# Releasing the attention units behind the first memory step, pacing them by a ScalarE clock, moving the softmax statistics off the SP queue and loading the group weights in one row

## The chip, the cores and the metric

The kernel runs on one core of a Trainium2 chip. The metric is the device time of one execution in microseconds (us); the time before is the median of three runs.

The engines are named as the profile names them: PE (TensorE, matrix multiplications), PEld (its weight loads), DVE (VectorE), ACT (ScalarE), POOL (GpSimd) and SP (SyncE, which only issues DMAs). A DMA stands on the queue of the engine that issues it: SPq, ACTq or POOLq. A queue issues in order, and an engine that reaches a DMA whose source is not ready waits there.

## The reference, cut to what matters

One layer of a decoder, 1024 positions of width 1024, in float32. The change lies in its first sub-layer:

```python
a = rmsnorm(h, g_mix[l])
proj = a @ w_in[l]                      # q, k, v, the gMLP's u and v, two gate logits
for gi, (win, dil) in enumerate(DIL_GROUPS):        # 3 groups of 4 heads, dilation 1, 4, 16
    o, lse = dilated_causal_window_attention(q[:, :, gi], k[:, :, gi], v[:, :, gi], slopes[gi], win, dil)
...
alpha = jax.nn.softmax(jnp.stack(lses), axis=0)     # weights of the three groups
y_attn = jnp.sum(alpha[..., None] * outs, axis=0)
y_sgu = spatial_gating(uv, w_sgu_spatial[l], b_sgu_spatial[l], g_sgu[l])
merged = gates[:, :, 0] * (y_attn @ w_branch_attn[l]) + gates[:, :, 1] * (y_sgu @ w_branch_sgu[l])
h = h + merged @ w_out[l]
```

The later sub-layers (cross-attention into 256 memory tokens, whose keys and values need `m @ w_kv_cross`, and a SwiGLU block) are computed by lines that the change leaves alone. Only the product with w_kv_cross is computed early, in the stretch that matters here.

## The kernel before, in words

Products that must be exact to float32 are done as three fp32r matmuls of a high and a low half (`mm3`, L168 to L171). `split` makes the halves: ACT writes the high one (L137), DVE the low one (L140).

**The order of the work** is written by the class `Order` (L40). A main generator yields (cost, latency) pairs, and its costs move a clock `now`. Up to four side chains are live; a chain may take its next step when `now` has reached the time that its last step's latency set. All engines' instructions are issued in the order so made, inside `tc.manual_schedule()` too, so that an engine that waits holds up all that stands behind it on that engine.

**The stretch from 443 to 606 us** of the span holds this work, by its PSUM tiles:
- memory keys and values, `mem_kv` (L1074 to L1100): steps 0 and 1 are `psk`, steps 2 and 3 `psv`, 96 matmuls of 256 columns each.
- attention, `attn_it` (L785 to L840): one unit is a few score blocks `psS` (L796); per block a DVE reduction with the bias (L805) and an ACT exponential in place in `T` (L807); transposes `psE` (L812), copied to `ET` by ACT and DVE in turn (L816, L818); products with v, `psO` (L827), copied to `oT` by ACT (L839). There are three groups of two head pairs. `spawn_attn` (L843) puts all units in a queue.
- `stats(g)` (L961 to L982), after the last unit of group g: two transposes `pst` (L969) of the row maxima and denominators, a DVE copy `stT` (L970), two stores to the scratch tensor `sc_d` (L974), each with four loads back as `stat` (L977), in another layout, all on SP, then POOL copies into `comb` (L981).
- `combine` (L984 to L1014): weights of the groups on DVE (L988 to L999, with one ACT exponential, L993), stored as `wt_d` (L1000); then per head pair three broadcasts `wbc` over the partitions, one half on ACTq and one on POOLq (L1006), and three multiplications of `oT` on DVE (L1007), two additions (L1008, L1009) and a split into `yAh` and `yAl`.
- the gMLP: `sgu_start` and `sgu_load` (its weights, `sguc` and `wsf`, and the scaled v, `sv`), `spatial` (L929 to L953, tile `psm`, with loads `u`), and its projection `branch_sgu` (L1018 to L1033, tile `psb`, four steps `jj` of 48 matmuls, each with gate loads `mg`).
- `branch_attn` (L1036 to L1051): tile `psa`, which needs `yAh` and `yAl`, so it stands behind `combine`; its gate loads are `sig` (L1041).

`order.join("attn%d")` lets the queued units run out. It stands behind the second `branch_sgu` step.

Of the kernel before, what the change touches and what calls it, by code (L numbers as in the profile page):

```python
# [15 lines left out]
P = 128  # L16
# [19 lines left out]
class Order:  # L36

    def __init__(self, limit):
        self.now = 0.0
        self.limit = limit
        self.live = []
        self.waiting = []
# [3 lines left out]

    def _advance(self, th):  # L50
        try:
            cost, lat = next(th[1])
            self.now += cost
            th[0] = self.now + lat
        except StopIteration:
            self.live.remove(th)

# [28 lines left out]
def tile_hybrid_dilated_attn_sgu_gated_block(  # L86
# [25 lines left out]
    nc = tc.nc  # L112
# [11 lines left out]
    def H(name, dt=F32, shape=(P, 1024)):  # L124
        return heap.tile(list(shape), dt, name=name, tag="h")
# [124 lines left out]
    order = Order(4)  # L250
# [310 lines left out]
    def load_bias():  # L561
        two = big.tile([P, 2, 1024], F32, name="bias", tag="b")
        nc.gpsimd.dma_start(two, bias_tab[:, :2048].rearrange("p (g c) -> p g c", g=2))
        one = H("bias2", shape=(P, 512))
        nc.gpsimd.dma_start(one, bias_tab[:, 2048:2560])
        bias.extend([two[:, 0], two[:, 1], one])
# [104 lines left out]
    qk, vts, oT = {}, {}, {}  # L671
# [109 lines left out]
    def attn_it(g, pr, it, st):  # L781
        if (g, pr) not in oT:
            oT[g, pr] = H("oT")
        q, k = qk[g, pr]
        vt = vts[g]  # L785
        T = W("T")
        lay = []
        c = 0
        cost = 0.0
        for hh in range(2):  # L790
            S_hd = PS("psS")
            cs = c
            for (b, kbs) in it:
                n = len(kbs) * P
                S_ps = S_hd[:, c - cs:c - cs + n]
                nc.tensor.matmul(S_ps, lhsT=q[hh * HD:(hh + 1) * HD, b * P:(b + 1) * P],  # L796
                                 rhs=k[hh * HD:(hh + 1) * HD, kbs[0] * P:kbs[0] * P + n], start=True, stop=True)
                lay.append((b, kbs, hh, c, n, S_ps))
                c += n
                cost += n / P * 0.216  # L800
        for (b, kbs, hh, c0, n, S_ps) in lay:
            h = 2 * pr + hh
            col = (g * HPG + h) * 8 + b
            bt = bias[g][:, h * P:(h + 1) * P] if g == 2 else bias[g][:, h * 256 + 256 - n:(h + 1) * 256]
            nc.vector.tensor_tensor_reduce(T[:, c0:c0 + n], S_ps, bt, op0=ALU.add, op1=ALU.min,  # L805
                                           scale=1.0, scalar=3e38, accum_out=nmx[:, col:col + 1])
            nc.scalar.activation(T[:, c0:c0 + n], T[:, c0:c0 + n], AF.Exp, bias=nmx[:, col:col + 1], scale=-1.0,  # L807
                                 accum_out=den[:, col:col + 1])
        yield cost, 3.0
        E_ps = PS("psE")  # L810
        for j in range(c // P):
            nc.tensor.transpose(E_ps[:, j * P:(j + 1) * P], T[:, j * P:(j + 1) * P], ident)  # L812
        ET = W("ET")
        st["n"] += 1
        if st["n"] % 2:
            nc.scalar.activation(ET[:, :c], E_ps[:, :c], AF.Copy)  # L816
        else:
            nc.vector.tensor_copy(ET[:, :c], E_ps[:, :c])  # L818
        yield c / P * 0.107, 1.8
        for (b, kbs, hh, c0, n, _) in sorted(lay, key=lambda l: l[0]):  # L820
            q4, ob = divmod(b, 4)
            if q4 not in st:
                st[q4] = [PS("psO"), 0]
            O = st[q4][0]
            for j, kb in enumerate(kbs):
                v = vt[kb // 4][:, (kb % 4) * 256 + (2 * pr + hh) * HD:(kb % 4) * 256 + (2 * pr + hh + 1) * HD]
                nc.tensor.matmul(O[hh * HD:(hh + 1) * HD, ob * P:(ob + 1) * P], lhsT=v,  # L827
                                 rhs=ET[:, c0 + j * P:c0 + (j + 1) * P],
                                 start=(j == 0), stop=(j == len(kbs) - 1))
            st[q4][1] += 1  # L830
            if st[q4][1] == 8:
                d = DIL[g]
                nr = max(1, d // 2)
                o = oT[g, pr].rearrange("p (i r) -> p r i", r=d)
                if d == 1:
                    o = o[:, :, q4 * 512:(q4 + 1) * 512]
                else:
                    o = o[:, q4 * nr:(q4 + 1) * nr, :]
                nc.scalar.activation(o, O.rearrange("p (r i) -> p r i", r=nr), AF.Copy)  # L839
        yield c / P * 0.2, 0.0  # L840

    def spawn_attn():
        its = [(g, pr) for g in range(GROUPS) for pr in range(2)]  # L843
# [76 lines left out]
    def sgu_load():  # L920
        for half in range(2):
            nc.gpsimd.dma_start(vt_s[half], sv_d[4 * half:4 * half + 4].rearrange("b i c -> i b c"))
# [32 lines left out]
    sc_d = dram.tile([GROUPS, 2, HPG, S], F32, name="sc_d")  # L955
    wt_d = dram.tile([GROUPS, HPG, S], F32, name="wt_d")

    def comb(i):
        return consts_["comb"][:64, i * 64:(i + 1) * 64]

    def stats(g):  # L961
        while order.busy("attn%d" % g):
            yield 0.0, 1.0
        if g == 0:
            consts_["comb"] = H("comb")
        ps = PS("pst")
        stT = W("stT")
        for w_, t in enumerate((nmx, den)):
            nc.tensor.transpose(ps[:32, w_ * P:(w_ + 1) * P], t[:, g * 32:(g + 1) * 32], ident)  # L969
        nc.vector.tensor_copy(stT[:32, :256], ps[:32, :256])  # L970
        d = DIL[g]
        stat = W("stat")
        for w_ in range(2):
            nc.sync.dma_start(sc_d[g, w_].rearrange("h (b q) -> (h b) q", q=P), stT[:32, w_ * P:(w_ + 1) * P])  # L974
            src = sc_d[g, w_].rearrange("h (r c i) -> h c r i", r=d, i=64 // d)
            for h in range(HPG):
                nc.sync.dma_start(  # L977
                    stat[h * 16:(h + 1) * 16, w_ * 64:(w_ + 1) * 64].rearrange("p (r i) -> p r i", r=d), src[h])
        yield 0.22, 0.0
        for w_ in range(2):  # L980
            nc.gpsimd.tensor_copy(comb(3 * w_ + g).rearrange("p (i r) -> p i r", r=d),  # L981
                                  stat[:64, w_ * 64:(w_ + 1) * 64].rearrange("p (r i) -> p i r", r=d))  # L982

    def combine():  # L984
        while order.busy("stats"):
            yield 0.0, 1.0
        low, tot = comb(6), comb(7)
        nc.vector.tensor_tensor(low, comb(0), comb(1), op=ALU.min)  # L988
        nc.vector.tensor_tensor(low, low, comb(2), op=ALU.min)
        for g in range(3):  # L990
            nc.vector.tensor_sub(comb(g), low, comb(g))
        n_, dn_ = [consts_["comb"][:64, i * 192:(i + 1) * 192] for i in range(2)]
        nc.scalar.activation(n_, n_, AF.Exp)  # L993
        nc.vector.tensor_mul(dn_, dn_, n_)
        nc.vector.tensor_add(tot, comb(3), comb(4))
        nc.vector.tensor_add(tot, tot, comb(5))
        nc.vector.reciprocal(low, tot)
        for g in range(3):
            nc.vector.tensor_mul(comb(g), comb(g), low)  # L999
            nc.scalar.dma_start(wt_d[g].rearrange("h (c i) -> (h c) i", i=64), comb(g))  # L1000
        for pr in range(2):
            for g in range(3):
                t = H("wbc")
                for hh in range(2):
                    src = wt_d[g, 2 * pr + hh:2 * pr + hh + 1, :]
                    (nc.scalar, nc.gpsimd)[hh].dma_start(t[hh * HD:(hh + 1) * HD, :], src.to_broadcast([HD, S]))  # L1006
                nc.vector.tensor_mul(oT[g, pr], oT[g, pr], t)  # L1007
            nc.vector.tensor_add(oT[0, pr], oT[0, pr], oT[1, pr])  # L1008
            nc.vector.tensor_add(oT[0, pr], oT[0, pr], oT[2, pr])  # L1009
            y = H("yAh", F32R), H("yAl", F32R)  # L1010
            split(oT[0, pr], *y)
            yA.append(y)
            yield 0.0, 0.0
# [522 lines left out]
    def main():  # L1536
# [15 lines left out]
        with tc.manual_schedule():  # L1552
            load_qk(0, 0)
            load_bias()
            yield from mem_kv(0)
            sgu_load()
            yield from mem_kv(1)
            load_qk(0, 1)
            order.spawn(sgu_start(), key="sgu")
            yield from mem_kv(2)  # L1560
            spawn_attn()
            yield from mem_kv(3)
        sgu_norm()
        order.join("sgu")
        yield from spatial()
        for jj in range(2):
            yield from branch_sgu(jj)
        for g in range(GROUPS):
            order.join("attn%d" % g)
        for jj in range(2, 4):  # L1570
            yield from branch_sgu(jj)
        order.join("combine")
        yield from branch_attn()
# [73 lines left out]
```

## Time and profile before

| what | value |
|---|---|
| median of three runs | 1486.52 us (1485.7 to 1486.54) |
| the profiled execution's own time | 1485.01 us |
| its span | 1483.2 us |
| PE busy | 1445.8 us, 97% of the span |
| DVE, ACT, POOL busy | 993.5, 609.2, 143.4 us |
| DMA moved | 211.78 MB, mean 143 GB/s |
| chain that ended last | PE 84%, DVE 7%, DMA 5%, ACT 2% |

The span is the time from the first to the last instruction of the profiled execution. The chain is followed back from the last instruction, at each step to what released it. A share of the span is an average over stages: the stretch of this change is 163 us of 1483. The stretch's rows stand in the section on rows.

### The profile page before, as it was taken

Reading aid. Unit: us, or ns where it says so; the run is one execution under the profiler, and the core shown is the slowest. Engines: PE = TensorE matmul, PEld = TensorE weight load, DVE = VectorE, ACT = ScalarE, POOL = GpSimd, SP = SyncE. Lnnn points to the kernel's source line nnn. Section 1 sums busy time; section 2 is a strip of 40 time slices with the busy share of each in tenths; the row PEclk is TensorE's granted clock in tenths of the full one; section 3 lists DMA queues with packets and bytes.
Section 4 is the critical chain, followed back from the end, with each engine's and each line's share of the span. In section 5 each row is a group of like instructions: output and inputs, shape, how many; then the busy total and the mean of one; then the engine's idle time right before and its main releaser. Section 6 shows DMA issues by size and latency. Waiting matters only on the chain.

```text
span 1483.2 us, 19504 instructions
## 1 busy us (share of the span) xinstructions
PE 1445.8 (97%) x7375; PEld 1210.7 (82%) x7375; DVE 993.5 (67%) x1855; ACT 609.2 (41%) x1150; POOL 143.4 (10%) x166
## 2 busy tenths in 40 slices
PE   8999999999998999899999999999999999999997
PEld 8899888888887768687888888888888888888876
DVE  7786555555546855898677896666666663876596
ACT  4245233343335771135456752222222221454463
POOL 5300000000012112100000000110110002200030
PEclk9999999999999999999999999999999999999999
DMA  6224333793379247532211313885874225943342
GB/s 214 65 91 129 115 114 114 208 244 108 108 237 311 85 173 185 161 115 68 72 53 62 114 58 119 213 209 143 219 176 129 80 84 184 377 149 93 107 149 78
DMA packets 162897, 211.78 MB, mean 143 GB/s; under 512 B 9150, under 2 KB 110258, under 8 KB 162676
## 3 DMA queue, kind: packets, MB, share of 16 engines
q1 hardware_dynamic: 134304, 127.09, 27.1%
q0 software_dynamic: 22640, 68.98, 16.8%
q10 hardware_dynamic: 5860, 14.47, 3.0%
q8 instruction: 58, 0.95, 0.3%
q14 instruction: 35, 0.29, 0.1%
HBM read 168.43 MB, written 73.55 MB: 163 GB/s over the span
## 4 chain that ended last, share of the span: by engine, by line
PE 84%; DVE 7%; DMA 5%; ACT 2%; issue 1%; POOL 0%; SPq 0%; ACTq 0%; POOLq 0%; DVEq 0%
PE psb L390 20%; PE psc L390 13%; PE psg L390 13%; PE psx L1165 8%; PE psy L1165 8%; PE psv L170 1%; PE psv L169 1%; PE psv L171 1%; DVE wl L140 1%; DMA wbc<-wt_d 1%; PE psb L469 1%; PE psq L171 1%; PE psq L170 1%; PE psq L169 1%; DVE nq L204 1%
## 5 line engine op out<-in xcount | busy, mean ns | idle before, releaser
L137 ACT ACTIVATE wh<-wst 128x1024 fp32r<-128x1024 f32 (+1 forms) x213 | 178.7, 840 | 348.2 <-PE psg L390 244.3
L140 DVE TENSOR_TENSOR wl<-wst,wh 128x512 fp32r<-128x512 f32 (+1 forms) x209 | 205.1, 983 | 82.2 <-ACT wh L137 82.2
L390 PE MATMUL psg<-A,wh 128*128 128x512 f32 x592 | 182.5, 389 | 0.0
L390 PEld LDWEIGHTS psg<-A,wh 128*128 128x128 f32 x592 | 111.1, 188 | 22.9
L390 PE MATMUL psg<-A,wl 128*128 128x512 f32 x296 | 115.2, 389 | 0.0
L390 PE MATMUL psc<-S,t 128*128 128x512 f32 x444 | 106.6, 389 | 0.0
L390 PEld LDWEIGHTS psc<-S,t 128*128 128x128 f32 x444 | 83.4, 188 | 17.3
L1165 PE MATMUL psx<-wh 128*128 128x512 f32 x240 | 93.9, 393 | 3.1 <-DVE h L1177 3.1
L1165 PE MATMUL psx<-wl,wh 128*128 128x512 f32 x240 | 94.4, 393 | 0.6 <-DVE wl L140 0.6
L1165 PE MATMUL psx<-wh,wl 128*128 128x512 f32 x240 | 94.0, 393 | 0.0
L390 PE MATMUL psc<-S,wh 128*128 128x512 f32 x296 | 91.4, 390 | 0.0
L390 PE MATMUL psb<-S,wh 128*128 128x512 f32 x296 | 91.3, 390 | 0.0
L390 PE MATMUL psb<-S,t2h 128*128 128x512 f32 x296 | 91.2, 389 | 0.0
L140 DVE TENSOR_TENSOR wl<-hm,wh 128x512 fp32r<-128x512 f32 x77 | 55.9, 726 | 50.3 <-ACT wh L137 50.2
L390 PE MATMUL psb<-A,t2h 128*128 128x512 f32 x288 | 88.8, 390 | 0.6 <-DVE v L1423 0.6
L137 ACT ACTIVATE wh<-hm 128x512 fp32r<-128x512 f32 x77 | 48.4, 630 | 95.0 <-PE psy L1165 45.8
L411 DVE TENSOR_TENSOR u<-p,psb 128x512 f32<-128x512 f32 x37 | 25.4, 687 | 90.1 <-PE psb L390 90.1
L1165 PE MATMUL psy<-wh 128*128 128x512 f32 x180 | 70.2, 390 | 0.3 <-ACT wh L137 0.3
L1165 PE MATMUL psy<-wh,wl 128*128 128x512 f32 x180 | 70.1, 389 | 0.0
L1165 PE MATMUL psy<-wl,wh 128*128 128x512 f32 x180 | 70.1, 389 | 0.0
L414 DVE TENSOR_TENSOR v<-p,psc 128x512 f32<-128x512 f32 x37 | 25.4, 687 | 64.8 <-PE psc L390 64.8
L390 PEld LDWEIGHTS psg<-A,wl 128*128 128x128 f32 x296 | 55.6, 188 | 11.6
(354 smaller groups left out, 3395.8 us busy)
## 6 DMA issues: line engine op xcount, KB each, us to landing
wst<-in_w_gate_up_dram SPq DMA_DIRECT2D x44, 512.0 KB, 4.9
wst<-in_w_in_dram SPq DMA_DIRECT2D x42, 512.0 KB, 4.9
hm_d<-hmf SPq DMA_DIRECT2D x44, 256.0 KB, 4.4
hm<-hm_d POOLq DMA_DIRECT2D x22, 512.0 KB, 9.3
wst<-wdT SPq DMA_DIRECT2D x20, 512.0 KB, 3.7
wdT<-in_w_down_dram POOLq DMA_DIRECT2D x12, 768.0 KB, 9.1
sig_d<-act ACTq DMA_DIRECT2D x16, 512.0 KB, 3.7
wst<-in_w_down_dram SPq DMA_DIRECT2D x15, 512.0 KB, 5.4
```

The source lines that it names most:

```text
L137: i = nc.scalar.activation(hi, src, AF.Copy)
L140: (eng or nc.vector).tensor_sub(lo, src, hi.bitcast(F32))
L169: nc.tensor.matmul(ps, lhsT=lh, rhs=rh, start=(i == 0), stop=False)
L170: nc.tensor.matmul(ps, lhsT=lh, rhs=rl, start=False, stop=False)
L171: nc.tensor.matmul(ps, lhsT=ll, rhs=rh, start=False, stop=(i == n - 1))
L204: nc.vector.scalar_tensor_tensor(q[:, c:c + 1], y[:, c:c + 1], ms[i][:, c:c + 1], y[:, c:c + 1], op0=ALU.mult, op1=ALU.mult)
L390: nc.tensor.matmul(ps, lhsT=l, rhs=r, start=first and k == 0 and i == 0, stop=k == 3 and i == 2, skip_group_check=not first)
L411: nc.vector.tensor_add(u, p1, b)
L414: nc.vector.tensor_add(v, p1, c)
L469: nc.tensor.matmul(p, lhsT=l, rhs=r, start=first and t % 2 == 0 and k == 0 and i == 0, stop=k == 3 and i == 2, skip_group_check=not first ...
L1165: nc.tensor.matmul(bank[t], lhsT=l, rhs=r, start=fresh and i == 0, stop=k == kp - 1 and i == 2, skip_group_check=s_ not in (0, 1, 3))
```

## The change

There are four parts.

1. `Order` gets a second clock, `act`. A step may yield a third number, the ACT time that it brings. The clock then moves on by 1.1 times that number (from `now`, if that is later), and the chain's next step may not come before the clock plus 1.0. The exponentials bring 0.3 + 0.107 per 128 columns each, an `ET` copy on ACT 0.107 per 128 columns + 0.13, an `oT` copy 0.6 or 1.1. The two latencies in `attn_it` fall from 3.0 to 2.4 and from 1.8 to 1.5.
2. `spawn_attn` is called behind memory step 0 and not behind step 2; `sgu_start` is spawned ahead of step 0 and `sgu_load` comes behind step 1. The join on the attention groups moves from behind the second `branch_sgu` step to behind the first.
3. The statistics' stores and loads leave SP: POOL for groups 0 and 1; for group 2 ACT for the maxima and POOL for the denominators.
4. `combine` issues all six broadcasts in a row ahead of all multiplications.

```diff
--- before.py
+++ after.py
@@ -38,8 +38,10 @@
     def __init__(self, limit):
         self.now = 0.0
+        self.act = 0.0
         self.limit = limit
         self.live = []
         self.waiting = []
@@ -49,9 +51,12 @@
 
     def _advance(self, th):
         try:
-            cost, lat = next(th[1])
+            cost, lat, *act = next(th[1])
             self.now += cost
             th[0] = self.now + lat
+            if act:
+                self.act = max(self.act, self.now) + 1.1 * act[0]
+                th[0] = max(th[0], self.act + 1.0)
         except StopIteration:
             self.live.remove(th)
 
@@ -806,7 +811,7 @@
                                            scale=1.0, scalar=3e38, accum_out=nmx[:, col:col + 1])
             nc.scalar.activation(T[:, c0:c0 + n], T[:, c0:c0 + n], AF.Exp, bias=nmx[:, col:col + 1], scale=-1.0,
                                  accum_out=den[:, col:col + 1])
-        yield cost, 3.0
+        yield cost, 2.4, sum(0.3 + n / P * 0.107 for (_, _, _, _, n, _) in lay)
         E_ps = PS("psE")
         for j in range(c // P):
             nc.tensor.transpose(E_ps[:, j * P:(j + 1) * P], T[:, j * P:(j + 1) * P], ident)
@@ -816,7 +821,8 @@
             nc.scalar.activation(ET[:, :c], E_ps[:, :c], AF.Copy)
         else:
             nc.vector.tensor_copy(ET[:, :c], E_ps[:, :c])
-        yield c / P * 0.107, 1.8
+        yield c / P * 0.107, 1.5, (c / P * 0.107 + 0.13) * (st["n"] % 2)
+        evac = 0.0
         for (b, kbs, hh, c0, n, _) in sorted(lay, key=lambda l: l[0]):
             q4, ob = divmod(b, 4)
             if q4 not in st:
@@ -837,7 +843,8 @@
                 else:
                     o = o[:, q4 * nr:(q4 + 1) * nr, :]
                 nc.scalar.activation(o, O.rearrange("p (r i) -> p r i", r=nr), AF.Copy)
-        yield c / P * 0.2, 0.0
+                evac += 0.6 if d == 1 else 1.1
+        yield c / P * 0.2, 0.0, evac
 
     def spawn_attn():
         its = [(g, pr) for g in range(GROUPS) for pr in range(2)]
@@ -971,10 +978,11 @@
         d = DIL[g]
         stat = W("stat")
         for w_ in range(2):
-            nc.sync.dma_start(sc_d[g, w_].rearrange("h (b q) -> (h b) q", q=P), stT[:32, w_ * P:(w_ + 1) * P])
+            q = nc.gpsimd if g < 2 else (nc.scalar, nc.gpsimd)[w_]
+            q.dma_start(sc_d[g, w_].rearrange("h (b q) -> (h b) q", q=P), stT[:32, w_ * P:(w_ + 1) * P])
             src = sc_d[g, w_].rearrange("h (r c i) -> h c r i", r=d, i=64 // d)
             for h in range(HPG):
-                nc.sync.dma_start(
+                q.dma_start(
                     stat[h * 16:(h + 1) * 16, w_ * 64:(w_ + 1) * 64].rearrange("p (r i) -> p r i", r=d), src[h])
         yield 0.22, 0.0
         for w_ in range(2):
@@ -998,13 +1006,16 @@
         for g in range(3):
             nc.vector.tensor_mul(comb(g), comb(g), low)
             nc.scalar.dma_start(wt_d[g].rearrange("h (c i) -> (h c) i", i=64), comb(g))
+        wbc = {}
         for pr in range(2):
             for g in range(3):
-                t = H("wbc")
+                t = wbc[g, pr] = H("wbc")
                 for hh in range(2):
                     src = wt_d[g, 2 * pr + hh:2 * pr + hh + 1, :]
                     (nc.scalar, nc.gpsimd)[hh].dma_start(t[hh * HD:(hh + 1) * HD, :], src.to_broadcast([HD, S]))
-                nc.vector.tensor_mul(oT[g, pr], oT[g, pr], t)
+        for pr in range(2):
+            for g in range(3):
+                nc.vector.tensor_mul(oT[g, pr], oT[g, pr], wbc[g, pr])
             nc.vector.tensor_add(oT[0, pr], oT[0, pr], oT[1, pr])
             nc.vector.tensor_add(oT[0, pr], oT[0, pr], oT[2, pr])
             y = H("yAh", F32R), H("yAl", F32R)
@@ -1552,22 +1563,21 @@
         with tc.manual_schedule():
             load_qk(0, 0)
             load_bias()
+            order.spawn(sgu_start(), key="sgu")
             yield from mem_kv(0)
-            sgu_load()
-            yield from mem_kv(1)
             load_qk(0, 1)
-            order.spawn(sgu_start(), key="sgu")
-            yield from mem_kv(2)
             spawn_attn()
-            yield from mem_kv(3)
+            for step in range(1, 4):
+                yield from mem_kv(step)
+                if step == 1:
+                    sgu_load()
         sgu_norm()
         order.join("sgu")
         yield from spatial()
-        for jj in range(2):
-            yield from branch_sgu(jj)
+        yield from branch_sgu(0)
         for g in range(GROUPS):
             order.join("attn%d" % g)
-        for jj in range(2, 4):
+        for jj in range(1, 4):
             yield from branch_sgu(jj)
         order.join("combine")
         yield from branch_attn()
```

The change moves instructions on all engines. In the rows below, names that repeat have their buffer numbers left out, and line numbers of the changed kernel are up to 11 higher. The first place is PE where attention starts, before:

```order
L169 MATMUL psv<-wh,mT_3674 128x256
L170 MATMUL psv<-wl,mT_3674 128x256
L171 MATMUL psv<-wh,mT_3675 128x256
L796 MATMUL psS<-k,q 128x128 x2
L796 MATMUL psS<-k,q 128x256 x6
L169 MATMUL psv<-wh,mT_3674 128x256
L170 MATMUL psv<-wl,mT_3674 128x256
L171 MATMUL psv<-wh,mT_3675 128x256
L169 MATMUL psv<-wh,mT_3674 128x256
```

and in the changed kernel:

```order
L174 MATMUL psk<-mT_3674,wh 128x256
L175 MATMUL psk<-mT_3675,wh 128x256
L176 MATMUL psk<-mT_3674,wl 128x256
L801 MATMUL psS<-k,q 128x128 x2
L801 MATMUL psS<-k,q 128x256 x6
L817 MATMUL psE<-ident,T 128x128 x2
L174 MATMUL psk<-mT_3674,wh 128x256
L175 MATMUL psk<-mT_3675,wh 128x256
L176 MATMUL psk<-mT_3674,wl 128x256
L174 MATMUL psk<-mT_3674,wh 128x256
```

The scores `psS` now stand behind 69 `psk` matmuls, while 27 `psk` and all 96 `psv` come between the units; before, they stood behind all of `psk` and 84 of `psv`.

The second place is POOL around the copies of group 0's statistics, before (`q`, `k`, `v` are loads for a later head pair, `u` is a load for `spatial`):

```order
L936 DMA u<-u_d 128x1024 x2
L981 COPY comb<-stat 64x64
L936 DMA u<-u_d 128x1024
L981 COPY comb<-stat 64x64
L754 DMA q<-qk_d 128x1024
L754 DMA k<-qk_d 128x1024
L767 DMA v<-v_d 128x1024 x2
```

and in the changed kernel:

```order
L982 DMA sc_d<-stT 32x128
L985 DMA stat<-sc_d 16x64 x4
L982 DMA sc_d<-stT 32x128
L985 DMA stat<-sc_d 16x64 x4
L989 COPY comb<-stat 64x64 x2
L759 DMA q<-qk_d 128x1024
L759 DMA k<-qk_d 128x1024
L772 DMA v<-v_d 128x1024 x2
L943 DMA u<-u_d 128x1024
```

A store, its four loads, the other store, its four loads and the two copies of group 0 now stand in a row on POOL, ahead of the loads of group 2's first pair and of `u`.

The third place is ACT from its last `oT` copies to the split of the merged attention, before:

```order
L839 ACTIVATE oT<-psO 128x4x128 x2
L137 ACTIVATE wh<-wst 128x1024
L993 ACTIVATE comb<-comb 64x192
L1000 DMA wt_d<-comb 64x64 x3
L1006 DMA wbc<-wt_d 64x1024 x3
L137 ACTIVATE wh<-wst 128x1024
L137 ACTIVATE yAh<-oT 128x1024
L1006 DMA wbc<-wt_d 64x1024 x3
```

and in the changed kernel:

```order
L845 ACTIVATE oT<-psO 128x4x128 x2
L142 ACTIVATE wh<-wst 128x1024
L982 DMA sc_d<-stT 32x128
L985 DMA stat<-sc_d 16x8x8 x4
L1001 ACTIVATE comb<-comb 64x192
L142 ACTIVATE wh<-wst 128x1024
L1008 DMA wt_d<-comb 64x64 x3
L1015 DMA wbc<-wt_d 64x1024 x6
L142 ACTIVATE wh<-wst 128x512
L142 ACTIVATE yAh<-oT 128x1024 x2
```

The broadcasts stand in one row behind the stores of the weights, and both `yAh` come behind them; a store and four loads of group 2's maxima are new on ACT. On DVE at the same place, before:

```order
L818 COPY ET<-psE 128x512 x2
L970 COPY stT<-pst 32x256
L1033 TENSOR_TENSOR mg<-mg,psb 128x512 x2
L140 TENSOR_TENSOR wl<-wst,wh 128x1024
L989 TENSOR_TENSOR comb<-comb 64x64
```

and in the changed kernel:

```order
L823 COPY ET<-psE 128x512
L1044 TENSOR_TENSOR mg<-mg,psb 128x512 x2
L145 TENSOR_TENSOR wl<-wst,wh 128x1024
L977 COPY stT<-pst 32x256
L1044 TENSOR_TENSOR mg<-mg,psb 128x512 x3
L997 TENSOR_TENSOR comb<-comb 64x64
```

Two gate products and a split of a weight (`wl`) now stand ahead of the copy `stT` of the last group.

By counts of the PE order, 51 of the 192 `psb` matmuls now stand ahead of group 2's `pst` and 141 behind it (27 and 165 before).

## Rows read from the trace of the kernel before

**Rows 1.** The page, first part: busy us, share and instructions of each engine.

```profile
PE 1445.8 (97%) x7375; PEld 1210.7 (82%) x7375; DVE 993.5 (67%) x1855; ACT 609.2 (41%) x1150; POOL 143.4 (10%) x166
```

**Rows 2.** Stretches: length, busy us of PE, PEld, DVE, ACT, POOL, clock, DMA, GB/s.

```profile
443.00:505.00 62.00, 57.32 (x495) 48.05 (x495) 44.23 (x119) 40.30 (x106) 8.76 (x15) 1.00 0.65 221
505.00:533.00 28.00, 26.67 (x245) 19.44 (x243) 20.86 (x82) 21.28 (x71) 10.00 (x17) 1.00 0.64 224
533.00:557.00 24.00, 21.09 (x176) 15.10 (x173) 10.88 (x68) 18.41 (x73) 0.56 (x2) 0.93 0.22 75
557.00:601.30 44.30, 38.07 (x169) 31.19 (x167) 27.60 (x41) 6.07 (x7) 11.82 (x19) 0.98 0.75 203
570.00:582.00 12.00, 12.00 (x55) 9.94 (x54) 7.97 (x9) 1.06 (x1) 5.45 (x9) 1.00 1.00 234
601.30:606.50 5.20, 5.20 (x13) 4.09 (x14) 2.42 (x4) 0.00 (x0) 0.53 (x1) 0.53 0.91 303
```

**Rows 3.** Chain of waits, 443 to 543 us: start, us, what; PE's pieces of work.

```profile
444.98 0.12 PE psk L169
...
489.87 0.91 PE psm L941 x8
...
525.13 1.06 PE psS L796 x8
526.20 0.59 PE psO L827 x8
526.79 0.59 PE psE L812 x4
...
531.67 1.19 PE psS L796 x16
...
540.17 0.23 PE psb L171
```

**Rows 4.** Waits of PE, 443 to 606 us: total, times, longest.

```profile
PE psa L169 <- ACT yAh L137: 6.2, 1, 6.2
PE psE L812 <- ACT T L807: 3.7, 3, 2.1
PE psO L827 <- ACT ET L816: 2.3, 3, 1.7
```

**Rows 5.** Chain of waits, 540 to 606 us: the last group's statistics and what follows.

```profile
543.61 3.19 ACT T L807 x16
...
556.57 0.34 PE pst L969 x2
...
557.44 2.37 DMA sc_d<-stT
...
561.20 1.61 DMA stat<-sc_d
...
570.70 7.64 DMA wbc<-wt_d
...
583.03 10.99 DMA wbc<-wt_d
...
600.15 1.07 ACT yAh L137
...
601.26 1.22 PE psa L169 x2
```

**Rows 6.** DMA issues of the whole span: KB, us to landing; a tiny load of POOL's, at its start.

```profile
rowc<-in_b_gate_dram POOLq DMA_DIRECT2D x1, 8.0 KB, 6.1
```

**Rows 7.** By line, DVE 500 to 606 us, POOL 440 to 606: shape, count, busy, mean ns.

```profile
L140 DVE TENSOR_TENSOR wl<-wst,wh 128x1024 fp32r<-128x1024 f32 x2 | 2.4, 1222 | 0.2 <-ACT wh L137 0.2
L1033 DVE TENSOR_TENSOR mg<-mg,psb 128x512 f32<-128x512 f32 x16 | 10.8, 682 | 10.6 <-PE psb L171 10.6
L1006 POOL DMA_DIRECT2D wbc<-wt_d x6 | 3.1, 525 | 4.5 <-DMA wt_d<-comb 4.3
```

**Rows 8.** Instructions of tile stat: count, ns min, median and max, first and last start.

```profile
L981 POOL COPY comb<-stat x6: 278/299/1051, 512.1 to 564.8; 64x64 f32<-64x64 f32 x6
```

## The prediction

> **What bounds the kernel now.** I read the page first: PE is busy for 97% of the span [rows 1], so only PE's gaps and its own work are there to be won. The stretches show where the gaps are. From 443 to 557 us PE idles 62.00 - 57.32 = 4.7, then 1.3, then 2.9 us, in all 8.9; from 557 to 601.3 it idles 6.2; behind that it runs 5.2 us at clock 0.53, which is near the lower of its two levels (1.2 of 2.4 GHz), and that costs 5.2 x 0.47 = 2.4 us [rows 2]. The waits of PE name what it waits for: 6.2 us for yAh, once, and in attention 3.7 us for the exponentials and 2.3 us for the copies ET, both ACT's [rows 4]. The chain shows the row of exponentials (3.19 us) that stands between two pieces of attention, and then the last group's path: transposes pst at 556.57, store, loads, broadcasts in two parts (7.64 and 10.99 us), yAh at 600.15, psa at 601.26 [rows 5].
>
> So two things decide: how late pst of the last group comes (I call that time T0), and how long the path from T0 to yAh is against the PE work that covers it.
>
> **PE's work up to T0.** Both kernels do the same matmuls between the first psk (443.0) and the first psa. By the chain's pieces [rows 3]: 192 psk and psv x 0.12 = 23.0; 140 psE x 0.59/4 = 20.6; 280 psO x 0.59/8 = 20.6; psS 104 x 1.19/16 + 88 x 1.06/8 = 19.4; 64 psm x 0.91/8 = 7.3; 192 psb x 0.23 = 44.2; ten small transposes, some 1.5. Sum 136.6. In the order before, 98.5 us of this stand ahead of T0; T0 came 556.57 - 443.0 = 113.6 after the start, so PE lags its own work by 15.1 us. Of that 8.9 is idle; 24 x 0.07 = 1.7 is the clock of 0.93 from 533 to 557 [rows 2]; the rest, 4.5, is small gaps between unlike matmuls.
>
> In the new order 24 more psb stand ahead of T0 and everything else as before, so 98.5 + 24 x 0.23 = 104.0 us of work. T0 will be 443.0 + 104.0 + the new lag.
>
> **The new lag, part by part.**
> - Attention's early start: the scores stand behind 69 psk, and 27 psk and 96 psv (14.8 us of work) come as filler between the units; before only 12 psv did (1.4 us). The 4.7 us of idle ahead of 505 lie where units follow each other with little between; I let 1.5 of it stay. Bounds: 0 and 4.7.
> - The ACT clock: it adds no work. It spreads the exponentials, so that rows like the one at 543.61 [rows 5] are broken up with psb between. The idle and the clock loss from 533 to 557 are 2.9 + 1.7 = 4.6; I leave 0.6. Bounds: 0, and 4.6 if ACT is as late as before.
> - The statistics on POOL: a chain of store, landing, four issues, landing of the last, second store and four issues, landing, two copies. At 0.525 us an issue on POOL [rows 7], and with landings of 2.37 and 1.61 as on SP [rows 5], group 0 takes 10 x 0.525 + 2 x 2.37 + 1.61 + 0.6 = 12.2 us. The buffer of stat is taken next by T of the first unit of group 1's second pair, whose DVE reduction waits for POOL's copy; 11.0 us of PE work lie between group 0's pst and that unit's scores. Behind the same row on POOL stand the loads of group 2 and u. I put both at 2.0 us of PE. Bounds: 0, and what the first rival gives. Group 1's statistics have some 10 us of slack, so they cost nothing; without that cover it would be the same wait again.
> - The 1.3 idle of 505 to 533 goes into the 2.0; the small gaps, 4.5, stay.
>
> Sum: 1.5 + 0.6 + 2.0 + 4.5 = 8.6. So T0 = 443.0 + 104.0 + 8.6 = 555.6, 1 us earlier than before, with 24 more psb done.
>
> **From T0 to yAh.** Before: 601.22 - 556.57 = 44.7 us [rows 5]. After:
> - On DVE, two mg products and a wl split stand ahead of stT; some of it runs before T0; I take 0.69 + 1.22 = 1.9 late, plus the copy's 0.4 [rows 7].
> - The two stores go on two queues at once; landing 2.4, four issues of 0.525, landing 1.6, two copies of 0.3: 6.7. The path of the weights (DVE, one exponential, wt_d) took 5.0 and 0.4 more in waits and stays so. First broadcast at T0 + 2.3 + 6.7 + 5.4 = T0 + 14.4; it was T0 + 12.4. The edit on SP is a loss here, of 2 us, and is paid from cover.
> - Twelve broadcasts in a row are 12 x 0.25 MiB = 3.1 MB. When broadcasts moved alone (570 to 582) the chip moved 234 GB/s with DMA at 1.00 [rows 2]: 13.4 us, plus 2 until the first bytes: T0 + 29.8. The second set before stood behind yAh on ACTq and landed last at 594.02, T0 + 37.4 [rows 5].
> - Then one multiplication, one split, one addition, one mg, one addition in order: 1.2 + 1.2 + 1.2 + 0.7 + 1.2, then yAh 1.07 and semaphores: 7.2 [rows 5, 7]. The other head pair's work lies beside the transfers. yAh is done at T0 + 37.0.
>
> PE's cover is 141 psb x 0.23 + 0.3 = 32.7 us (before 38.3). So PE waits 4.3 us in place of 6.2, and psa starts at 555.6 + 37.0 = 592.6, against 601.26: 8.7 us earlier. The clock drop behind the wait I keep as it is: the wait is still there. Everything later stands in the same order, so I carry nothing further on.
>
> The profiled execution took 1485.01 us; it stands 1.5 below the median. 1485.01 - 8.7 = 1476.3, and on the scale of the median 1477.8.
>
> **The rivals.**
>
> *POOL's small transfers land late.* On record for tiny POOL loads is 6.1 us, at the start of the span, beside the first big loads [rows 6]; on SP the same stores and loads land in 2.37 and 1.61 [rows 5]. At 6.1, group 0's chain is 2 x 3.7 + 4.5 = 11.9 us longer and DVE, then PE, waits that long at the unit that reuses the buffer; group 2's is 3.7 + 4.5 = 8.2 longer, with no cover left. 8.7 + 2.0 - 11.9 - 8.2 = -9.4: 1496 us, slower. Each microsecond of a landing counts five times, so the sign turns at 1.7 us over SP's landings. For it: one POOL copy of the statistics took 1051 ns where 299 is the median [rows 8], so something holds POOL at times. Against it: the start of the span is a busy place, and POOL's issues of broadcasts took an even 525 ns [rows 7].
>
> The Trainium skill, page "SBUF — State Buffer", section "SBUF: two separate sides", speaks against this part of the change: DMAs issued by GpSimd need descriptors that it writes, and it cannot write them while VectorE holds the port pair that they share, so the transfer waits for the VectorE instruction to end. Its example, about 620 ns alone and 3100 ns under such an instruction, would as an estimate add 2.5 us to a landing, and the time would be some 1490 us. The trace has the slow copy for it, and no POOL transfer so small beside DVE work that could show the landing.
>
> *The lag stays and the tail gets little.* ACT's total in attention is unchanged; the clock only orders. If the 4.6 us of the last attention stretch stay and the start keeps 3 of its 4.7, the lag is 3 + 4.6 + 2 + 4.5 = 14.1, and the gain 8.7 - 5.5 = 3.2; if gate loads push among the broadcasts by 2 us, 1.2. So 1483 to 1485. For it: T of the last group needs the same 3.19 us rows of ACT. This is also the case in which the pacing does not do what it says.
>
> *It works more fully.* No new wait on POOL and no idle at the start: the lag is near 5; the broadcasts run at the 303 GB/s that the rows behind show [rows 2], 10.4 us. The path is then T0 + 34, near the cover of 32.7: gain 8.7 + 3.6 + 3.0 = 15.3, and with the clock partly kept 16: 1470.5.
>
> **How the numbers follow.** About 3 us, 0.2%, is what a measurement of this kernel can tell from no change. The forecast (gain of 5 to 12) has 0.50; the little gain 0.20, of which a third is over 3 us; the full one 0.15; late POOL landings 0.15, of which a third ends within 3 us of before and the rest slower. Faster 0.50 + 0.15 + 0.07 = 0.72, same 0.13 + 0.05 = 0.18, slower 0.10. The range leaves out half of the late landings and the top of the full case: 1470.5 to 1487.0.
>
> **What would show it.** Right: the first psS some 11 us earlier than before; the row of 16 exponentials gone; pst of the last group at 554 to 557; twelve broadcasts landing one behind another from T0 + 19 to T0 + 30; psa near 592 with a wait for yAh of some 4 us. Wrong: a DVE wait on POOL's copies of several us in the middle of attention; landings of sc_d or stat over 4 us on POOLq; a psa wait above 8 us; psa later than 600; or a slower stretch behind 607, where I expect no change.

## The result: 1% slower, and the profile after

The changed kernel takes 1501.68 us (median of 4 runs, 1499.63 to 1504.85) against 1486.53 beside it: ratio 1.0102, 95% interval 1.0081 to 1.0122. The forecast of 1477.8 us, with a range to 1487.0, was wrong in sign. The profiled execution took 1501.55 us.

The page of the changed kernel answers to [rows 1]:

```profile
PE 1451.6 (97%) x7375; PEld 1218.7 (81%) x7375; DVE 993.1 (66%) x1855; ACT 609.3 (41%) x1150; POOL 154.0 (10%) x191
...
PE 81%; DVE 7%; DMA 7%; ACT 2%; issue 2%; POOL 1%; ACTq 0%; SPq 0%; POOLq 0%; DVEq 0%
```

PE has as many instructions as before and the same share of a span that is 16 us longer (1499.6 us): a share of 97% hides that. Its busy time is 5.8 us longer, as a slow clock stretches it (the stretches below). The chain says more: DMA has 7% of it in place of 5%. The stretches of the changed kernel, columns as in [rows 2], cut at group 2's transposes (579.5) and at the first psa matmul that needs the second head pair's yAh (618.3; it stood at 601.26 before, and the forecast put it at 592.6):

```profile
443.00:470.00 27.00, 17.91 (x104) 15.83 (x103) 6.98 (x22) 8.29 (x21) 3.85 (x6) 0.76 0.92 337
470.00:505.00 35.00, 31.77 (x317) 26.72 (x315) 22.59 (x82) 22.85 (x74) 0.00 (x0) 0.99 0.16 47
505.00:533.00 28.00, 23.65 (x201) 20.66 (x198) 17.70 (x52) 19.81 (x56) 8.53 (x18) 0.88 0.63 206
533.00:579.50 46.50, 42.99 (x315) 32.90 (x316) 28.87 (x113) 30.71 (x102) 13.40 (x24) 0.93 0.42 140
579.50:618.30 38.80, 33.39 (x147) 26.97 (x145) 24.48 (x36) 4.53 (x6) 13.21 (x23) 0.99 0.69 190
```

The first 27 us hold the largest loss: 9.1 us of PE idle and a mean clock of 0.76. Before, PE idled 2.0 us there at full clock:

```profile
443.00:470.00 27.00, 25.05 (x199) 23.64 (x198) 19.12 (x39) 14.30 (x26) 7.70 (x13) 1.00 0.95 320
```

What PE waited for from 443 to 640 us in the changed kernel (answers to [rows 4]), and, from ACT's own waits, what stands behind psk's wait:

```profile
PE psO L833 <- DVE ET L823: 7.5, 5, 2.5
PE psS L801 <- DVE nmx L810: 5.5, 1, 5.5
PE psa L174 <- ACT yAh L142: 3.2, 1, 3.2
PE psk L174 <- ACT wh L142: 2.9, 1, 2.9
...
ACT wh L142 <- DMA wst<-in_w_kv_cross_dram: 15.6, 2, 11.0
```

The chain (start, us, what) shows how these hang together:

```profile
430.34 33.57 DMA wst<-in_w_kv_cross_dram
463.91 0.02 issue
463.94 1.06 ACT wh L142
465.00 0.02 issue
465.02 0.03 DVE wl L145
465.06 1.11 issue
466.17 0.28 DVE T L810
466.45 0.02 DVE nmx L810
466.47 0.04 issue
466.51 1.22 PE psS L801 x2
```

One weight of the memory was issued at 430 and landed at 463.9. ACT and DVE, in order, stood at its split, and the first unit's reduction stood behind that split: the first scores were computed from 458 to 461, and nothing used them before 466. SP's queue tells why it was issued at 430 (start, us until the last issue, line, what). The changed kernel:

```profile
386.92 16.68 SPq L152 DMA_DIRECT2D wst<-in_w_kv_cross_dram  x2
412.02 11.18 SPq L1072 DMA_DIRECT2D mem<-in_mem_dram  x2
423.30 0.40 SPq L912 DMA_DIRECT2D wsf<-in_w_sgu_spatial_dram  x1
429.44 0.33 SPq L918 DMA_DIRECT2D sguc<-in_b_sgu_spatial_dram  x1
429.86 43.59 SPq L152 DMA_DIRECT2D wst<-in_w_kv_cross_dram  x6
```

The kernel before:

```profile
386.38 30.29 SPq L147 DMA_DIRECT2D wst<-in_w_kv_cross_dram  x4
416.76 0.53 SPq L1061 DMA_DIRECT2D mem<-in_mem_dram  x1
```

With sgu_start spawned ahead of memory step 0, both mem loads, wsf and sguc stand ahead of the third weight, and sguc goes out at 429.4 only. Before, the third and fourth weight went out at 405.4 and 416.3, and mem, wsf and sguc came behind them. (The mem loads are another chain's, not sgu_start's; why they too come ahead is not shown.) What SP waited for at these loads from 405 to 435 us, in the changed kernel:

```profile
SPq L1072 <- PE psb L395: 10.5, 1, 10.5
SPq L1072 <- PE psc L395: 8.4, 1, 8.4
SPq L918 <- PE psc L395: 5.7, 1, 5.7
```

So, by the profile, mem (L1072) and sguc (L918) stood on the queue until PE's matmuls of the stage before (L395) had ended, and the weights stood behind them. In the kernel before, SP has none of these three waits there.

The tail, from group 2's pst at 579.5, in the chain:

```profile
593.45 2.21 DMA wt_d<-comb
595.66 3.93 issue
...
600.09 8.03 DMA wbc<-wt_d
...
617.22 1.07 ACT yAh L142
618.29 0.04 issue
618.33 1.22 PE psa L174 x2
```

From T0 to psa it is 618.3 - 579.5 = 38.8 us; the forecast said 37.0, and before it was 44.7.

### The profile page after: what moved, and what is told of

The parts are those of the page before. It is cut to its first block, busy times and chain, and to the rows that moved or that the text cites. A ratio compares the mean times of both kernels' runs of the same rounds, so it can differ in the third digit from the quotient of the medians.

```text
span 1499.6 us, 19486 instructions
## 1 busy us (share of the span) xinstructions
PE 1451.6 (97%) x7375; PEld 1218.7 (81%) x7375; DVE 993.1 (66%) x1855; ACT 609.3 (41%) x1150; POOL 154.0 (10%) x191
## 4 chain that ended last, share of the span: by engine, by line
PE 81%; DVE 7%; DMA 7%; ACT 2%; issue 2%; POOL 1%; ACTq 0%; SPq 0%; POOLq 0%; DVEq 0%
PE psb L395 19%; PE psg L395 13%; PE psc L395 13%; PE psy L1176 8%; PE psx L1176 7%; DMA wst<-in_w_kv_cross_dram 2%; DVE wl L145 2%; PE psv L175 1%; PE psv L174 1%; PE psv L176 1%; PE psb L474 1%; PE pso L175 1%; PE pso L176 1%; PE pso L174 1%; DVE nq L209 1%
## 5 line engine op out<-in xcount | busy, mean ns | idle before, releaser
L395 PE MATMUL psg<-A,wh 128*128 128x512 f32 x592 | 182.5, 389 | 0.0
L395 PEld LDWEIGHTS psg<-A,wh 128*128 128x128 f32 x592 | 111.1, 188 | 23.2
L395 PE MATMUL psg<-A,wl 128*128 128x512 f32 x296 | 115.1, 389 | 0.0
L395 PE MATMUL psc<-S,t 128*128 128x512 f32 x444 | 106.7, 389 | 0.0
L395 PEld LDWEIGHTS psc<-S,t 128*128 128x128 f32 x444 | 83.3, 188 | 17.3
L395 PE MATMUL psc<-S,wh 128*128 128x512 f32 x296 | 91.4, 390 | 0.0
L395 PE MATMUL psb<-S,wh 128*128 128x512 f32 x296 | 91.2, 389 | 0.0
L395 PE MATMUL psb<-S,t2h 128*128 128x512 f32 x296 | 91.1, 389 | 0.0
L395 PE MATMUL psb<-A,t2h 128*128 128x512 f32 x288 | 88.9, 390 | 0.8 <-DVE v L1434 0.8
L395 PEld LDWEIGHTS psb<-S,t2h 128*128 128x128 f32 x296 | 55.6, 188 | 11.6
```

The source lines that it names most:

```text
L395: nc.tensor.matmul(ps, lhsT=l, rhs=r, start=first and k == 0 and i == 0, stop=k == 3 and i == 2, skip_group_check=not first)
```

## The experiments

My first theory was that the weights are late, and that POOL's earlier loads, which fill the DMA engines, make them so. The rival was the one of the prediction: POOL's statistics. The first four kernels each make one part of the change in the kernel before.

**Only the release** (with sgu_start, sgu_load and the join):

```diff
+            order.spawn(sgu_start(), key="sgu")
             yield from mem_kv(0)
-            sgu_load()
-            yield from mem_kv(1)
             load_qk(0, 1)
-            order.spawn(sgu_start(), key="sgu")
-            yield from mem_kv(2)
             spawn_attn()
...
```

> Only the early release of attention, with sgu_start and sgu_load moved and the join moved; the statistics, the broadcasts and the clock are as before. Theory (the memory weights come late: they stand behind mem, wsf and sguc on SPq and share full DMA engines with POOL's loads): 1496 to 1506 us, ACT waits of over 10 us for in_w_kv_cross between 440 and 470. Rival (POOL's statistics make the loss): within 4 us of 1486.5.

Measured: 1536.48 us, ratio 1.0334 (1.0303 to 1.0364). Worse than either said. ACT's waits for the weights are there, 14.1 us, but PE's largest wait is a new one:

```profile
PE psb L169 <- ACT yS L137: 40.3, 1, 40.3
```

Without the clock all attention, and combine behind it, stands ahead of the gMLP in the order. ACT waits at yAh for combine's products (19.4 us) and for a gate load (13.8 us), the copies yS stand behind it and come at 604 us, and psb, which should cover that wait, waits for yS. What the clock does in the full change is to put psb between the units. This kernel has the early sgu_start in it, so it does not price the release alone.

**Only the statistics off SP** (the edit `q = nc.gpsimd if g < 2 else (nc.scalar, nc.gpsimd)[w_]`):

> Only the statistics moved off SPq, everything else as before. Theory: landings on POOLq are near SP's (1.9 us median in the changed kernel), so only issues of 0.5 and DVE's wait for POOL's copies cost: 1486 to 1491 us. Rival (POOL's statistics make the loss): 1496 us or more.

Measured: 1486.23 us, ratio 0.9998 (0.9979 to 1.0016). The theory holds and the rival falls.

**Only the row of broadcasts** (all six wbc issued ahead of the first multiplication):

> Only the six broadcasts in one row, everything else as before. Theory: last broadcast lands some 28 us behind the last group's pst and not 37, the wait of 6.2 us for yAh falls under the 38 us of cover and with it the slow clock of 2.4 us: 1478 to 1482 us. Rival (broadcasts are bound by bandwidth or by gate loads): 1484 to 1487 us.

Measured: 1475.58 us, ratio 0.9930 (0.9903 to 0.9957). The last group's pst stands at 557.5, within 1 us of before, and PE does not wait for yAh at all. This part gains more than the theory said, and of the four it is the only one that gains by itself.

**Only the clock** (the act clock and the shorter latencies):

> Only the clock for ScalarE and the shorter latencies, everything else as before. Theory: it adds no work and spreads the exponentials; 1482 to 1488 us. Rival (the clock's order is what makes PE wait): 1492 us or more.

Measured: 1495.33 us, ratio 1.0064 (1.0040 to 1.0089): the rival holds, by PE's wait for yAh:

```profile
PE psa L173 <- ACT yAh L141: 13.7, 2, 7.1
```

The clock spreads the units: group 2's pst comes at 572.0 and not at 556.6, and psb, spent between the units, is missing behind it: 96 matmuls of psb stand there, where 165 stood before. So by itself it is an exchange of cover, not a gain.

**The changed kernel with sgu_start one step later.** The second four kernels take the changed kernel and undo something.

```diff
-            order.spawn(sgu_start(), key="sgu")
             yield from mem_kv(0)
+            order.spawn(sgu_start(), key="sgu")
```

> The changed kernel, with sgu_start spawned behind memory step 0 in place of ahead of it, so that four weights of the memory stand on SPq ahead of mem, wsf and sguc. Theory (POOL's early loads of group 1 fill the DMA engines; the place on SPq matters little): 1497 to 1502 us. Rival (the order on SPq is what makes the weights late): 1492 us or less, and ACT's wait of 15.6 us for in_w_kv_cross falls below 6.

Measured: 1474.08 us, ratio 0.9927 (0.9900 to 0.9953): 27.6 us below the changed kernel by the medians, 26 by the ratios. My theory that the place on SPq matters little falls; the rival holds. Its queue and its first stretch:

```profile
385.19 30.29 SPq L152 DMA_DIRECT2D wst<-in_w_kv_cross_dram  x4
```

```profile
443.00:470.00 27.00, 26.76 (x238) 21.98 (x236) 18.84 (x63) 18.51 (x55) 2.62 (x4) 1.00 0.76 285
```

PE idles 0.2 us where it idled 9.1, at full clock; ACT waits for no weight of the memory. pst of group 2 comes at 556.0, and psa starts at 590.9 without a wait. The edit moves more than the queue: by counts of the PE order, 39 psb now stand ahead of group 2's pst and 153 behind it (51 and 141 in the changed kernel).

**The changed kernel with group 1's loads on SPq** (behind weights, not ahead of them on POOL; `q_ = nc.sync if g == 1 else nc.gpsimd` in `load_qk`):

> The changed kernel, with the loads of q, k and v of group 1 issued on SPq behind weights of the memory, and not on POOL ahead of them. Theory (these loads take the DMA engines from the weights): ACT's wait for in_w_kv_cross falls from 15.6 to below 6 us and the time to 1488 to 1495 us. Rival (the weights are late because of their own issue): within 3 us of 1501.7.

Measured: 1496.17 us, ratio 1.0068 (1.0043 to 1.0093). Both expectations miss: ACT's wait for the weights falls from 15.6 to 8.6 us only, and the time by some 5 us, with intervals that overlap. So group 1's loads on POOL are at most a part of the delay.

**The changed kernel with the statistics back on SP:**

> The changed kernel with the statistics back on SPq. Theory: landings on POOLq are near SP's and DVE's wait of 5 us for POOL's copy is all there is to win: 1496 to 1502 us. Rival (POOL's statistics make a good part of the loss): 1492 us or less.

Measured: 1506.21 us, ratio 1.0139 (1.0110 to 1.0168). Both expectations miss: taking them off SPq helps there, if anything.

**The kernel before with the clock and the row:**

> The kernel before with the clock and the row of broadcasts only. Theory: the clock alone cost 9.4 us because it moves the last group's pst later and takes cover from the tail; with the row the tail is short enough, so most of that vanishes: 1474 to 1481 us. Rival (the two add up): 1484 to 1486 us.

Measured: 1487.43 us, ratio 1.0016 (1.0003 to 1.0030). My theory falls; the loss of the clock stays beside the gain of the row. PE still waits 7.7 us for yAh, as cover is what the clock takes.

The last four test that one line by itself, and what is left when it is mended. **The kernel before with that one line early:**

```diff
             load_bias()
+            order.spawn(sgu_start(), key="sgu")
             yield from mem_kv(0)
...
-            order.spawn(sgu_start(), key="sgu")
             yield from mem_kv(2)
```

> The kernel before with one line moved: sgu_start is spawned ahead of memory step 0, so that mem, wsf and sguc stand ahead of the third weight of the memory on SPq. Nothing else of the change is in it. Theory (this line is the cause of the loss): the third weight is issued near 430 us and not near 412, PE waits for psk's weights and the time is 1494 to 1503 us. Rival (it hurts only where attention's loads come early): within 4 us of 1485.

Measured: 1496.33 us, ratio 1.0060 (1.0038 to 1.0082). The theory holds: without any other part of the change this line costs 0.6%, and ACT waits as in the changed kernel. The third and fourth weight go out at 429.3 and 429.8 (not at 405.4 and 416.3), and the first stretch is as in the changed kernel:

```profile
ACT wh L137 <- DMA wst<-in_w_kv_cross_dram: 15.2, 4, 6.2
```

```profile
443.00:470.00 27.00, 18.77 (x118) 17.27 (x117) 11.21 (x19) 7.21 (x10) 5.00 (x8) 0.77 0.98 360
```

PE runs psk, psv, attention and psb in the same order as before (only sgu_start's own four transposes come earlier), so this run shows the line's cost with little else in it: 8.2 us of idle and 18.77 x 0.23 = 4.3 of slow clock, against 2.0 and none. The line costs more in the changed kernel (27.6 us), but not in this stretch, where the loss is nearly the same. The rest comes later, where the edit also changes the order of psb; what of it is the order's and what the late first unit's is not shown.

**Three edits of the version with sgu_start later:** statistics on SP, no row, and another order of the minimum (`min(comb(1), comb(2))` first), which keeps a step of combine from standing in the middle of attention on DVE.

> The version with sgu_start behind step 0, and the statistics back on SPq. Theory (the statistics' queue matters little): 1471 to 1478 us. Rival (on SPq they stand behind weights that wait, and attention waits for them): 1479 us or more.

Measured: 1475.02 us, ratio 0.9920 (0.9897 to 0.9944): no difference, so the theory holds. Beside the kernel before with the clock and the row (1.0016), this version has the release in addition: with the clock, and with sgu_start behind step 0, the release (and the moved join) wins back what the clock costs, some 13 us.

> The version with sgu_start behind step 0, with the broadcasts issued per head pair as before. Theory (the row shortens the tail by more than its cover is short): PE waits for yAh again and the time is 1480 to 1485 us. Rival (the earlier statistics are cover enough): within 3 us of 1474.

Measured: 1485.59 us, ratio 0.9989 (0.9971 to 1.0008). The wait is the theory's, the time just above its range. Without the row nothing is left of the gain: PE waits 5.2 us for yAh again. Release, clock and statistics together, with the line mended, are worth nothing that can be measured: the clock loses and the release wins about as much.

> The version with sgu_start behind step 0, with the minimum over the three groups taken in another order (groups 1 and 2 first, then 0), so that no step of combine can stand in DVE's order ahead of group 2's statistics. Theory: DVE's wait of some 4 us for POOL's copy in the middle of attention goes, and PE's 3.2 us behind it: 1469 to 1472 us. Rival (T's buffer waits for the same copy): within 2 us of 1474.

Measured: 1474.57 us, ratio 0.9920 (0.9890 to 0.9950). The rival holds; PE's wait of 3.1 us for a DVE copy ET is still there, so what it hangs on is not this step, and that is left open.

No version beats "sgu_start later" or "only the row" clearly: their intervals overlap, both some 11 us below before, and "only the row" is the smallest edit.

## Why the prediction was wrong

**The step that failed is the first bullet of the new lag**, "attention's early start". It spoke of PE's filler between the units and bounded the stretch ahead of 505 us by 0 and 4.7 us of idle. It never named the first line of the edit, sgu_start ahead of memory step 0, so its cost was nothing without a cover being named. No DMA that the moved step issues was counted against the queue that it is moved on: mem, wsf and sguc pass the third and fourth weight on SPq, sguc goes out at 429.4, and the weights behind it are issued at least 13 us later. By PE's own work (104.0 us ahead of T0) the lag was 579.5 - 443.0 - 104.0 = 32.5 us and not 8.6; these 24 us are nearly the whole miss of the time. Of the lag, 9.1 us of idle and 17.91 x 0.24 = 4.3 of slow clock, 13.4 in all, arise from 443 to 470; the bullet had 1.5 for all that lies ahead of 505. That the line alone makes this loss, the kernel before with that line early shows: 10.5 us more idle and slow clock than before in the same stretch, and 9.7 us of the time.

**The rest of the lag** came behind it. By the stretches, PE idles 3.2 + 4.4 + 3.5 us from 470 to 579.5, and the clock below 1.00 costs, on the busy time, 0.3 + 2.8 + 3.0. What made them is open, but for one wait of DVE, which was forecast at the wrong place:

```profile
DVE comb L996 <- POOL comb L989: 5.0, 1, 5.0
```

It is the first step of combine, which stands in DVE's order in the middle of attention and waits for group 1's statistics. I had given those 10 us of slack. How much of it PE felt is not shown: with the line mended, taking this step away changed nothing.

**The pacing** was rightly described as adding no work, and wrongly costed at 4 us of gain: alone it lost 9.4 us by lost cover. The version with the line mended comes near the forecast: T0 at 556.0 (forecast 555.6), the time 1474.08 (forecast 1477.8). That is luck in part. There 39 psb stand ahead of pst and not 51, so PE's work ahead of T0 is 98.5 + 12 x 0.23 = 101.3 us; its first psk already comes at 441.8, and from there the lag is 556.0 - 441.8 - 101.3 = 12.9 and not 8.6. The lag is over 4 us too long, and the shorter work and the earlier start hide that. The gain there is the row's, which also stood for most of the forecast's sum (7.7 of 8.7 us from T0 to psa): the row alone wins 10.4 us, at a T0 within 1 us of before.

**The tail** was right in kind and near in size: 38.8 us measured, 37.0 forecast. The last broadcast landed at 611.9, T0 + 32.4 (forecast T0 + 29.8): ACT and POOL issued no broadcast from 595.6 to 599.1 (the step "issue" in the chain has 3.93 us there), for a reason that the profile does not settle. From there the steps to the end of yAh took 6.4 us (forecast 7.2). The rate of the broadcasts was read from a stretch, 570 to 582, in which four gate loads were issued too, so there they did not move alone. The row by itself removes the wait of 6.2 us and the slow clock of 2.4 us behind it [rows 2, 4], together 8.6 of its 10.4 us.

**The rival of late landings on POOL** gave the right sign for a wrong reason. (By its own sum, 8.7 + 2.0 over five landings, the sign turns at 2.1 us and not at 1.7, and the estimate of 2.5 us a landing gives 1488 us and not 1490.) The statistics of the changed kernel, POOL's and ACT's loads and their landings together:

```profile
L985 POOL DMA_DIRECT2D stat<-sc_d x20: 484/512/548, 507.9 to 587.3; - x20
...
DMA to landing us min/median/max: 1.6/1.9/4.0
```

They land in 1.9 us by the median, while on SP before it was 1.6. The Trainium skill's page "SBUF — State Buffer", section "SBUF: two separate sides", warned of GpSimd's DMAs starving while VectorE holds the ports that they share; these landings do not show it at the size that its example has, and the measurement decides: the part alone is worth 0.9998.

**The rival of a lag that stays** was nearer in kind, and its price, 5.5 us of lag above the forecast's, was far too small: 23.9 measured.

## What to carry to other kernels

A line that spawns a small preparation earlier also moves its loads ahead of whatever stands on that queue: read the queue's order before and after, with the time at which each passed load's buffer comes free, before costing anything on the compute engines. In a kernel whose engines work in order, spreading a stage with filler spends the filler: what it gains in the stage is paid where that work covered a wait (here 9.4 us for the clock alone). Where several loads serve one row of uses, try issuing them together, ahead of the first use and of anything on that queue that waits for a result; here that was worth 10.4 us, more than the rest of the change.

## What the runs showed of the hardware

The third and fourth weight of the memory are loads of 512 KB on SPq, in rows of 512 bytes (128 columns of float32). Before, they landed in 5.2 and 3.9 us. In the changed kernel, issued at 429.9 and 430.3 among POOL's loads, they took 21.8 and 33.6 us (first line), and in the kernel before with the one line early 14.9 and 26.1 (second line):

```profile
DMA to landing us min/median/max: 21.8/27.7/33.6
DMA to landing us min/median/max: 14.9/20.5/26.1
```

POOL's loads of q and k, of the same 512 KB, took 10 and 12 us by the median in the changed kernel. From 448 to 464 us DMA's share is 0.9 or more in every slice. The queues in that stretch (packets, MB, share of the 16 engines; q0 is POOL's, q1 is SP's), in the changed kernel and then in the kernel before with the line early:

```profile
q0 software_dynamic: 1237, 4.50, 75.0%
q1 hardware_dynamic: 1285, 0.94, 18.7%
...
q0 software_dynamic: 1258, 4.49, 73.5%
q1 hardware_dynamic: 1179, 1.10, 20.6%
```

Both queues moved nearly as many packets, but SPq's hold 0.94 MB / 1285 = 0.7 KB on average and POOL's 4.50 MB / 1237 = 3.6 KB, so SPq moved 4.8 times fewer bytes. The Trainium skill's page "DMA: Bandwidth & Descriptors", section "Queues, rings and completion order", says that an engine takes the queues in turn, a packet from each. The near-equal counts agree with that if a packet of the profile is one of the page's, which can hold several descriptors; no run shows that, and none varied the size of the packets alone.
